# One rms per group applied to the branch product's sums instead of to the SSD rows

## The chip, the cores and the metric

The kernel runs on one core of a Trainium2 chip. The metric is the device time of one execution in microseconds (us). A core has TensorE (PE, matrix products into PSUM), VectorE (DVE), ScalarE (ACT), GpSimd (POOL) and SyncE (SP), whose queue issues the large DMA transfers. All engines work through their own instruction queues, and meet through semaphores.

## The reference

One layer of an encoder block on 256 tokens of width 1024, in float32. The input projection feeds a sparse-attention branch and a Mamba-2 (SSD) branch; both are gated, merged and projected, and a mixture of experts follows.

```python
y_ssd = ssd_chunked(xh, dt, A, bs, cs) + d_skip[:, None] * xh
y_ssd = gated_group_rmsnorm(y_ssd, z, ssd_norm)
merged = sigmoid(gate_a) * (y_attn @ w_attn_branch) + sigmoid(gate_b) * (y_ssd @ w_ssd_branch)
x = x + merged @ w_out
x = x + hier_moe(rmsnorm(x, ffn_norm), ...)

def gated_group_rmsnorm(y, z, g):
    yf = y * silu(z)
    yg = yf.reshape(*yf.shape[:-1], 4, 512)                  # 4 groups of 512 channels
    yg = yg * rsqrt(mean(yg * yg, axis=-1, keepdims=True) + EPS)
    return yg.reshape(yf.shape) * g
```

What matters here is the last function: each token has one root mean square (rms) per group of 512 channels, and the normed rows are multiplied by `w_ssd_branch` (2048 x 1024). The factor 1 / rms belongs to a token and a group, so it is the same for all 512 channels that a group brings into the product.

## The kernel before, in words

**Products in split halves.** Nearly every product up to the router is made with each float32 operand split into two parts of a shorter type, a hi part (ACT, `split_hi`, L152) and a lo part, the operand less its hi (`split_lo`, L156). A k-tile of 128 rows then takes three matmuls, hi x hi, hi x lo and lo x hi:

```python
PASSES = ((0, 0), (0, 1), (1, 0))
KSP = (0, 1, 0, 1)      # lo parts: k-tiles 0, 2 on DVE and 1, 3 on POOL, and so on
```

**Weights in chunks.** The weights stream through chunks of 8 k-tiles of 128 x 512 (or 128 x 256). `next_w()` keeps one chunk ahead: it puts the raw chunk on SP's queue in pieces of 512 KB and asks for the splits. The hi and lo pairs live in a ring of six buffers, so that splits run at most six k-tiles ahead of PE. `wide_chunk` (L294) makes one product of a wide chunk for both halves t of the tokens into two PSUM tiles, half 1 three k-tiles behind half 0.

**The SSD groups.** The four groups g of 512 channels come in two halves q of 256. While PE goes through the input-projection chunks of group g + 1, and in the end through two chunks of the attention branch (`ps_A`), it also makes the SSD products of group g: `ssd_x` and `ssd_e` prepare, `ssd_y` makes `py` on PE (L749, L752), adds the skip on DVE (L755) and multiplies by the gate (L756) into `yg`, squares it on ACT (L758) and sums the squares on POOL into `ysum` (L760 to L763). `ssd_tail` sums `ysum` over the partitions with `ps_n` on PE (L769), takes the power -1/2 (DVE L771, POOL L100), broadcasts 1 / rms over the partitions with a second product `ps_r` (PE, L775), multiplies `yg` by the norm's gain and by `ps_r` (DVE, L781, 16 in all), and splits the result into `yT` (ACT L783, DVE L784, 8 each), which is PE's stationary operand in the merge.

**The merge.** Four chunks of `w_ssd_branch`, for i (which two groups, 8 k-tiles) and c (which 512 output columns). Each gives two sums `ps_S`, one for each t, over all 8 k-tiles. DVE multiplies a sum by the gate (L832; the gate tile `tab[t, c][:, 1]` holds a tanh, and 1 is added on the way). For i = 0 POOL adds it to `tab[t, c][:, 0]`, which holds the gated attention product (L834); for i = 1 DVE adds (L836), PE transposes (L839), and ACT and DVE split into `mT` (L844, L845) for the output projection `ps_o`. The weight chunks are w31 to w34 in the merge, and w35 to w37 in the output projection.

**After that** come the norm, the router and 96 weight tiles of 1 MB for the experts (`we`), which `prefetch` (L270) puts on SP's queue as buffers come free, the first of them during the groups and the merge.

**Order.** The program is written in loops, and a scheduler then puts the instructions of each engine into one fixed order, by priorities (`HP` gives SSD steps theirs) and by its own estimates. A change in one place can therefore move instructions elsewhere in an engine's queue.

Of the kernel before, what the change touches and what calls it, by code (L numbers as in the profile page):

```python
# [11 lines left out]
F32 = mybir.dt.float32  # L12
# [8 lines left out]
P = 128  # L21
# [27 lines left out]
def block_kernel(ctx, tc, xin, idn, ngain, catt, cprep, cssd, cmoe, cwr, wsm, wwide, win, wgu, wdn, out, dbg=None):  # L49
# [633 lines left out]
    snorm = C("snorm")  # L683
    yT = [bigt([P, 2, 4, T], F32R, f"yT{g}") for g in range(4)]
# [53 lines left out]
    def ssd_y(g, q):  # L738
# [3 lines left out]
        st_[g, q, "yg"] = yg  # L742
# [3 lines left out]
        for h2 in range(2):  # L746
            py = paux.tile([P, T], F32, tag="x", name="py")
            for hh in range(2):
                pe.matmul(py[64 * hh:64 * hh + 64], lhsT=xdt[:, 0, 2 * h2 + hh, :], rhs=e0[h2][:, hh, :],  # L749
                          start=True, stop=False)  # L750
            for hh in range(2):
                pe.matmul(py[64 * hh:64 * hh + 64, P:T], lhsT=xdt[:, 1, 2 * h2 + hh, :],  # L752
                          rhs=e1[h2][:, hh, :], start=False, stop=True)
            ct = 4 * g + 2 * q + h2
            dve.scalar_tensor_tensor(yg[:, h2, :], xs[:, h2, :], hsk[:, ct:ct + 1], py, op0=ALU.mult, op1=ALU.add)  # L755
            dve.tensor_tensor(yg[:, h2, :], yg[:, h2, :], zs[:, h2, :], op=ALU.mult)  # L756
        sq = zs_t[g, q]
# [7 lines left out]
    def ssd_tail(g):  # L765
# [4 lines left out]
        r = ssd.tile([P, 2], F32, tag="nv", name="nv")  # L770
        dve.tensor_scalar(r, ps_n, 1.0 / 512, 4 * EPS, op0=ALU.mult, op1=ALU.add)  # L771
        power(r, r, None)
        ps_r = paux.tile([P, T], F32, tag="n", bufs=1, name="ps_r")
        for t in range(2):
            pe.matmul(ps_r[:, t * P:(t + 1) * P], lhsT=r[:, t:t + 1].to_broadcast([P, P]), rhs=ident,  # L775
                      start=True, stop=True)
        for q in range(2):
            yg = st_[g, q, "yg"]
            for b in range(2):
                ct = 4 * g + 2 * q + b  # L780
                dve.scalar_tensor_tensor(yg[:, b, :], yg[:, b, :], snorm[:, ct:ct + 1], ps_r, op0=ALU.mult, op1=ALU.mult)  # L781
            hl = yT[g][:, :, 2 * q:2 * q + 2]
            act.copy(hl[:, 0], yg)  # L783
            dve.tensor_sub(hl[:, 1], yg, hl[:, 0].bitcast(F32))  # L784
# [40 lines left out]

    for i in range(2):
        for c in range(2):
            ps = wide_chunk("S", yT[2 * i:2 * i + 2], LAG)
            for t in range(2):
                ta, tb = tab[t, c][:, 0], tab[t, c][:, 1]  # L830
                m = mo2.tile([P, 512], F32, tag="y", name="mg")
                dve.scalar_tensor_tensor(m, tb, 1.0, ps[t], op0=ALU.add, op1=ALU.mult)  # L832
                if i == 0:
# [477 lines left out]
```

## Time and profile before

| | |
|---|---|
| time, median of 3 runs | 583.62 us (583.45 to 583.9) |
| the profiled execution's own time | 585.1 us |
| its span in the profile | 583.3 us |
| PE busy | 552.6 us (95%), 3605 instructions |
| DVE busy | 330.9 us (57%), 689 |
| ACT busy | 271.8 us (47%), 633 |
| POOL busy | 239.5 us (41%), 254 |
| read from HBM | 157.54 MB, 272 GB/s over the span |

The shares are averages over stages that differ: the input projection and the attention up to about 185 us, the SSD groups up to 307.6, the merge up to 353, the output projection and router up to about 388, and then the experts. Matmuls are pipelined, so a busy PE is not PE at its peak; what its work costs is better read from one start to the next. Idle time of an engine that nobody waits for costs nothing.

### The profile page before, as it was taken

The page shows a single profiled execution, that of the slowest core. Times are in us where ns is not written, and L with a number is a line of the kernel's source. Part 1 is how long each engine was busy: PE and PEld are TensorE (multiplying, and loading weights), DVE is VectorE, ACT ScalarE, POOL GpSimd, SP SyncE. Part 2 cuts the span into 40 slices and gives each one's busy share as a digit, 9 for nine tenths or more (in the row PEclk, how much of TensorE's full clock was granted, in tenths as well). Part 3 has the DMA queues.
Part 4 walks back from the last instruction along what each step waited for, and adds up shares of the span by engine and source line. Part 5 has one row for each costly group of instructions (what it writes and reads, how often), then busy time and mean ns, then how long its engine had stood idle before and what let it go on. Part 6 is the DMA issues. An engine that isn't in the chain of part 4 may idle for free.

```text
span 583.3 us, 9898 instructions
## 1 busy us (share of the span) xinstructions
PE 552.6 (95%) x3605; PEld 400.6 (69%) x3605; DVE 330.9 (57%) x689; ACT 271.8 (47%) x633; POOL 239.5 (41%) x254
## 2 busy tenths in 40 slices
PE   8999989999999999999999999999998898988976
PEld 5878768798898999898878888964453452433512
DVE  3659975999996778989695657451111121111101
ACT  7567557757987877878764436410000000000001
POOL 4687584775844456656567745210000000000000
PEclk9999999999999999999999999999989997999989
DMA  7755244453435488645568589989999999999993
GB/s 272 250 162 169 103 147 146 144 174 124 128 122 186 149 323 334 217 149 185 208 194 300 177 307 389 405 344 417 419 417 408 420 417 421 409 415 421 420 407 123
DMA packets 35123, 159.27 MB, mean 273 GB/s; under 512 B 4096, under 2 KB 5760, under 8 KB 25856
## 3 DMA queue, kind: packets, MB, share of 16 engines
q1 hardware_dynamic: 33776, 157.30, 71.8%
q10 hardware_dynamic: 1296, 1.30, 0.7%
q8 instruction: 30, 0.49, 0.3%
q14 instruction: 21, 0.17, 0.1%
HBM read 157.54 MB, written 1.05 MB: 272 GB/s over the span
## 4 chain that ended last, share of the span: by engine, by line
PE 69%; DMA 12%; DVE 9%; issue 4%; POOL 3%; ACT 3%; SPq 0%; ACTq 0%; POOLq 0%; DVEq 0%
PE ps_S L294 8%; PE pgu L1037 6%; PE ps_xs L241 6%; PE ps_g L294 6%; DMA we<-wdn 5%; DMA we<-wgu 5%; PE ps_z L241 5%; PE py L1097 4%; PE ps_A L294 4%; PE acc L1112 4%; PE ps_g L1030 4%; PE ps_q L294 3%; PE ps_o L241 2%; PE ps_o L294 2%; PE ps_iq L294 2%
## 5 line engine op out<-in xcount | busy, mean ns | idle before, releaser
L156 POOL TENSOR_TENSOR w_hl<-w_raw,w_hl 128x512 fp32r<-128x512 f32 (+1 forms) x101 | 141.6, 1406 | 81.8 <-ACT w_hl L152 66.5
L152 ACT CAST w_hl<-w_raw 128x512 fp32r<-128x512 f32 (+1 forms) x212 | 125.7, 620 | 46.4 <-PE ps_S L294 18.5
L156 DVE TENSOR_TENSOR w_hl<-w_raw,w_hl 128x512 fp32r<-128x512 f32 (+1 forms) x111 | 100.4, 911 | 38.7 <-ACT w_hl L152 38.1
L1055 POOL TENSOR_TENSOR dc<-Dm,cmr 128x128 f32<-128x128 f32 x16 | 6.1, 401 | 143.5 <-DVE Dm L960 137.4
L1037 PE MATMUL pgu<-we,xg 128*32 128x512 f32 x512 | 60.2, 603 | 3.9 <-DMA we<-wgu 3.9
L241 PE MATMUL ps_z<-hT,w_hl 128*128 128x256 f32 x384 | 51.7, 286 | 0.0
L241 PE MATMUL ps_xs<-hT,w_hl 128*128 128x256 f32 x384 | 50.7, 285 | 0.0
L241 PEld LDWEIGHTS ps_z<-hT,w_hl 128*128 128x128 f32 x384 | 47.8, 190 | 2.0 <-issue 2.0
L241 PEld LDWEIGHTS ps_xs<-hT,w_hl 128*128 128x128 f32 x384 | 47.6, 191 | 2.1 <-issue 2.1
L294 PE MATMUL ps_g<-w_hl,gT 128*128 128x512 f32 x192 | 48.1, 399 | 0.0
L294 PE MATMUL ps_S<-w_hl,yT 128*128 128x512 f32 x192 | 44.6, 391 | 0.0
L1033 DVE TENSOR_TENSOR xg<-ps_g,cmoe 128x512 f32<-128x512 f32 (+2 forms) x18 | 11.3, 631 | 57.4 <-PE ps_g L1030 57.4
L1030 PEld LDWEIGHTS ps_g<-Dm,x_sb 128*128 128x128 f32 x256 | 31.0, 191 | 14.9 <-issue 9.7
L294 PEld LDWEIGHTS ps_g<-w_hl,gT 128*128 128x128 f32 x192 | 34.9, 188 | 9.3 <-DVE w_hl L156 1.0
L294 PEld LDWEIGHTS ps_S<-w_hl,yT 128*128 128x128 f32 x192 | 35.8, 188 | 7.4
L1037 PEld LDWEIGHTS pgu<-we,xg 128*32 128x32 f32 x512 | 15.1, 110 | 37.1 <-issue 26.1
L1097 PE MATMUL py<-we,aTt 128*32 128x512 f32 (+1 forms) x272 | 35.8, 616 | 3.8 <-DVE aTt L1083 2.1
L1108 ACT COPY y<-py 128x512 f32<-128x512 f32 (+1 forms) x9 | 4.8, 539 | 66.9 <-PE py L1097 66.9
L1075 DVE SCALAR_TENSOR_TENSOR ac<-th,pgu 128x256 f32<-128x256 f32 x8 | 3.4, 421 | 57.5 <-ACT th L1073 57.5
L1112 PE MATMUL acc<-y,dcT 128*128 128x512 f32 (+1 forms) x68 | 32.6, 606 | 0.9 <-DVE y L1110 0.8
L1030 PE MATMUL ps_g<-Dm,x_sb 128*128 128x128 f32 x256 | 33.4, 280 | 0.0
L1073 ACT ACTIVATE th<-pgu,rs 128x256 f32<-128x256 f32 x8 | 3.8, 474 | 55.1 <-PE pgu L1037 55.1
(296 smaller groups left out, 968.9 us busy)
## 6 DMA issues: line engine op xcount, KB each, us to landing
we<-wgu SPq DMA_DIRECT2D x55, 1024.0 KB, 13.8
w_raw<-wwide SPq DMA_DIRECT2D x60, 512.0 KB, 3.9
w_raw<-win SPq DMA_DIRECT2D x44, 512.0 KB, 3.9
we<-wdn SPq DMA_DIRECT2D x17, 1024.0 KB, 17.4
we<-wdn SPq DMA_DIRECT2D x28, 512.0 KB, 12.0
we<-wgu SPq DMA_DIRECT2D x18, 512.0 KB, 10.2
x_sb<-xin SPq DMA_DIRECT2D x2, 512.0 KB, 4.4
we<-wdn SPq DMA_DIRECT2D x4, 256.0 KB, 11.5
```

Of the source, the lines that this page charges most:

```text
L152: return act.copy(self.hl[i][:, 0], self.raw[i])
L156: return eng.tensor_sub(hl[:, 1], self.raw[i], hl[:, 0].bitcast(F32))
L241: pe.matmul(ps, lhsT=lhs[k][:, a], rhs=rhs[k][:, b], start=j == 0 and k == 0 and i == 0, stop=j == len(regions) - 1 and k == KD - 1 and i ...
L294: pe.matmul(ps[t], lhsT=lhs[t][k][:, a], rhs=w[k][:, b], start=k == 0 and i == 0, stop=k == KD - 1 and i == 2)
L1030: pe.matmul(ps[:, kk, :], lhsT=x1[:, t, (k + kk) * P:(k + kk + 1) * P], rhs=Dm[:, t].rearrange("p e j -> p (e j)"), start=t == 0, stop=t == 1)
L1033: dve.tensor_tensor(xg[:, ks, :], ps, fgain[:, ks].unsqueeze(2).to_broadcast([P, n, P]), op=ALU.mult)
L1037: i = pe.matmul(pgu[32 * e:32 * e + 32, :], lhsT=xg[:, k, 32 * e:32 * e + 32], rhs=wg[k][e], start=k == 0, stop=k == KD - 1, tile_position ...
L1055: pool.tensor_tensor(dc[:, t], Dm[:, t], cmr[:, t, 4 * q:4 * q + 4].unsqueeze(2).to_broadcast([P, 4, NSLOT]), op=ALU.mult)
L1073: act.activation(th, pgu[:, 0:256], AF.Tanh, scale=rs)
L1097: i_py = pe.matmul(py[32 * e:32 * e + 32, :], lhsT=aTt[:, f, 32 * e:32 * e + 32], rhs=wd[2 * n + f][e][:, c], start=f == 0, stop=f == 1, t ...
L1108: act.copy(y, py)
L1112: pe.matmul(acc[t][n][:, c], lhsT=dcT[:, t * P:(t + 1) * P], rhs=y, start=False, stop=q == 7 and c.stop == 512)
```

## The change

The rows of SSD enter the branch product without their 1 / rms. `ssd_y` makes the hi and lo parts straight from `yg` and the norm's gain, per 128 channels. `ssd_tail` keeps 1 / rms as `rg[:, g, t]`, one number for each token on its partition, and makes no broadcast. In the merge, each chunk's product is kept apart by group: two sums of 4 k-tiles in place of one of 8, the second in PSUM banks of the accumulators. DVE multiplies each by its `rg` and by the gate in one instruction, and POOL or DVE adds: 12 additions on POOL (4 before) and 4 on DVE (as before). So that one instruction can do it, the gate tiles get their 1 beforehand, by four instructions on POOL.

```diff
@@ -681,6 +681,7 @@
         dve.tensor_scalar(hsk, C("dskip"), 0.5, None, op0=ALU.mult)
 
     snorm = C("snorm")
+    rg = cst.tile([P, 4, 2], F32, name="rg")
     yT = [bigt([P, 2, 4, T], F32R, f"yT{g}") for g in range(4)]
 
 
@@ -739,7 +740,6 @@
         xs, zs, xdt = xs_t[g, q], zs_t[g, q], st_[g, q]
         e0, e1 = st_[g, q, "e"]
         yg = ssd.tile([P, 2, T], F32, tag="yg", name=f"yg{g}{q}", bufs=YB)
-        st_[g, q, "yg"] = yg
         if q == 0:
             st_[g, "ysum"] = ssd.tile([P, T], F32, tag="ysum", name="ysum", bufs=1)
         ysum = st_[g, "ysum"]
@@ -754,6 +754,13 @@
             ct = 4 * g + 2 * q + h2
             dve.scalar_tensor_tensor(yg[:, h2, :], xs[:, h2, :], hsk[:, ct:ct + 1], py, op0=ALU.mult, op1=ALU.add)
             dve.tensor_tensor(yg[:, h2, :], yg[:, h2, :], zs[:, h2, :], op=ALU.mult)
+
+        hl = yT[g][:, :, 2 * q:2 * q + 2]
+        for b in range(2):
+            ct = 4 * g + 2 * q + b
+            act.activation(hl[:, 0, b], yg[:, b], AF.Copy, scale=snorm[:, ct:ct + 1])
+            dve.scalar_tensor_tensor(hl[:, 1, b], yg[:, b], snorm[:, ct:ct + 1], hl[:, 0, b].bitcast(F32),
+                                     op0=ALU.mult, op1=ALU.subtract)
         sq = zs_t[g, q]
         act.activation(sq, yg, AF.Square)
         if q:
@@ -767,21 +774,9 @@
         ps_n = paux.tile([P, 2], F32, tag="n", bufs=1, name="ps_n")
         for t in range(2):
             pe.matmul(ps_n[:, t:t + 1], lhsT=ysum[:, t * P:(t + 1) * P], rhs=ones, start=t == 0, stop=t == 1)
-        r = ssd.tile([P, 2], F32, tag="nv", name="nv")
+        r = rg[:, g]
         dve.tensor_scalar(r, ps_n, 1.0 / 512, 4 * EPS, op0=ALU.mult, op1=ALU.add)
         power(r, r, None)
-        ps_r = paux.tile([P, T], F32, tag="n", bufs=1, name="ps_r")
-        for t in range(2):
-            pe.matmul(ps_r[:, t * P:(t + 1) * P], lhsT=r[:, t:t + 1].to_broadcast([P, P]), rhs=ident,
-                      start=True, stop=True)
-        for q in range(2):
-            yg = st_[g, q, "yg"]
-            for b in range(2):
-                ct = 4 * g + 2 * q + b
-                dve.scalar_tensor_tensor(yg[:, b, :], yg[:, b, :], snorm[:, ct:ct + 1], ps_r, op0=ALU.mult, op1=ALU.mult)
-            hl = yT[g][:, :, 2 * q:2 * q + 2]
-            act.copy(hl[:, 0], yg)
-            dve.tensor_sub(hl[:, 1], yg, hl[:, 0].bitcast(F32))
 
     def steps(g, names):
 
@@ -823,14 +818,32 @@
     xp = ctx.enter_context(tc.tile_pool(name="xp", bufs=NX, reuse_waits="tile"))
     pacc = ctx.enter_context(tc.tile_pool(name="pacc", bufs=1, space=PSUM, reuse_waits="tile"))
 
+    for t in range(2):
+        for c in range(2):
+            pool.tensor_scalar(tab[t, c][:, 1], tab[t, c][:, 1], 1.0, None, op0=ALU.add)
     for i in range(2):
         for c in range(2):
-            ps = wide_chunk("S", yT[2 * i:2 * i + 2], LAG)
-            for t in range(2):
+
+            w = pairs(next_w(), slice(0, 512))
+            src = pairs(yT[2 * i:2 * i + 2], slice(0, T))
+            pss = {}
+            for k in range(KD + LAG):
+                for t in range(2):
+                    kk = k - LAG * t
+                    if not 0 <= kk < KD:
+                        continue
+                    g = kk // 4
+                    if kk % 4 == 0:
+                        pss[t, g] = (pacc.tile([P, 512], F32, tag=f"acc{t}1", name="ps_S") if g
+                                     else pmm.tile([P, 512], F32, tag="mm", name="ps_S"))
+                    for a, b in PASSES:
+                        pe.matmul(pss[t, g], lhsT=src[kk][:, a, t * P:(t + 1) * P], rhs=w[kk][:, b],
+                                  start=kk % 4 == 0 and (a, b) == PASSES[0], stop=kk % 4 == 3 and (a, b) == PASSES[2])
+            for g, t in ((0, 0), (0, 1), (1, 0), (1, 1)):
                 ta, tb = tab[t, c][:, 0], tab[t, c][:, 1]
                 m = mo2.tile([P, 512], F32, tag="y", name="mg")
-                dve.scalar_tensor_tensor(m, tb, 1.0, ps[t], op0=ALU.add, op1=ALU.mult)
-                if i == 0:
+                dve.scalar_tensor_tensor(m, pss[t, g], rg[:, 2 * i + g, t:t + 1], tb, op0=ALU.mult, op1=ALU.mult)
+                if i == 0 or g == 0:
                     pool.tensor_add(ta, m, ta)
                     continue
                 dve.tensor_add(m, m, ta)
```

The scheduler then orders the engines anew. Three places of the new order follow.

PE around the last `ps_n`, in the merge. `yT_2054` and `yT_2055` are the first two groups before, `yT_2055` and `yT_2056` in the change. Before (28 merge matmuls stand ahead of the first row):

```order
L294 MATMUL ps_S<-w_hl,yT_2055 128x512 x8
L769 MATMUL ps_n<-ones,ysum 128x1 x2
L294 MATMUL ps_S<-w_hl,yT_2055 128x512 x12
L294 MATMUL ps_S<-w_hl,yT_2054 128x512 x12
L775 MATMUL ps_r<-ident,nv 128x128 x2
L294 MATMUL ps_S<-w_hl,yT_2055 128x512
L294 MATMUL ps_S<-w_hl,yT_2054 128x512 x6
```

and in the change (the first row is the first merge matmul):

```order
L840 MATMUL ps_S<-w_hl,yT_2055 128x512
L749 MATMUL py<-e_3810,xdt_3775 64x256 x2
L840 MATMUL ps_S<-w_hl,yT_2055 128x512 x3
L752 MATMUL py<-e_3810,xdt_3775 64x128 x2
L840 MATMUL ps_S<-w_hl,yT_2055 128x512 x20
L776 MATMUL ps_n<-ones,ysum 128x1 x2
L840 MATMUL ps_S<-w_hl,yT_2055 128x512 x4
L840 MATMUL ps_S<-w_hl,yT_2056 128x512 x24
L840 MATMUL ps_S<-w_hl,yT_2055 128x512 x16
```

The last `ps_n` follows 36 merge matmuls before and 24 in the change, and no `ps_r` comes after it.

POOL from the last power on. `w32` and `w33` are the second and third merge chunk; the number behind `hl` tells the k-tile buffers apart, and `tab_692`, `tab_694`, `tab_1004`, `tab_1006` are the merge's four tiles. Before:

```order
L100 TENSOR_TENSOR nv_3947<-nv_3947,mhalf_80 128x2
L834 TENSOR_TENSOR tab_692<-mg_4059,tab_692 128x512
L156 TENSOR_TENSOR w32_hl_3990<-w32_raw_3981,w32_hl_3990 128x512
L834 TENSOR_TENSOR tab_694<-mg_4062,tab_694 128x512
L156 TENSOR_TENSOR w32_hl_3992<-w32_raw_3983,w32_hl_3992 128x512
L156 TENSOR_TENSOR w33_hl_4074<-w33_raw_4065,w33_hl_4074 128x512
L156 TENSOR_TENSOR w33_hl_4076<-w33_raw_4067,w33_hl_4076 128x512
L834 TENSOR_TENSOR tab_1004<-mg_4147,tab_1004 128x512
L156 TENSOR_TENSOR w33_hl_4078<-w33_raw_4069,w33_hl_4078 128x512
L834 TENSOR_TENSOR tab_1006<-mg_4150,tab_1006 128x512
```

and in the change:

```order
L100 TENSOR_TENSOR rg_2054<-rg_2054,mhalf_80 128x2
L847 TENSOR_TENSOR tab_692<-mg_4050,tab_692 128x512
L847 TENSOR_TENSOR tab_694<-mg_4053,tab_694 128x512
L847 TENSOR_TENSOR tab_692<-mg_4056,tab_692 128x512
L156 TENSOR_TENSOR w32_hl_3977<-w32_raw_3968,w32_hl_3977 128x512
L156 TENSOR_TENSOR w32_hl_3979<-w32_raw_3970,w32_hl_3979 128x512
L847 TENSOR_TENSOR tab_694<-mg_4059,tab_694 128x512
L156 TENSOR_TENSOR w32_hl_3981<-w32_raw_3972,w32_hl_3981 128x512
L156 TENSOR_TENSOR w33_hl_4071<-w33_raw_4062,w33_hl_4071 128x512
L847 TENSOR_TENSOR tab_1004<-mg_4146,tab_1004 128x512
L847 TENSOR_TENSOR tab_1006<-mg_4149,tab_1006 128x512
L156 TENSOR_TENSOR w33_hl_4073<-w33_raw_4064,w33_hl_4073 128x512
```

The first three additions stand together ahead of two splits, and 6 of the 11 rows behind the power are additions, where 4 of 9 were.

POOL's next rows, up to the output projection's first splits (`w35`). Before:

```order
L156 TENSOR_TENSOR w33_hl_4080<-w33_raw_4071,w33_hl_4080 128x512
L156 TENSOR_TENSOR w34_hl_4162<-w34_raw_4153,w34_hl_4162 128x512
L156 TENSOR_TENSOR w34_hl_4164<-w34_raw_4155,w34_hl_4164 128x512
L156 TENSOR_TENSOR w34_hl_4166<-w34_raw_4157,w34_hl_4166 128x512
L156 TENSOR_TENSOR w34_hl_4168<-w34_raw_4159,w34_hl_4168 128x512
L156 TENSOR_TENSOR w35_hl_4274<-w35_raw_4265,w35_hl_4274 128x512
L156 TENSOR_TENSOR w35_hl_4276<-w35_raw_4267,w35_hl_4276 128x512
L156 TENSOR_TENSOR w35_hl_4278<-w35_raw_4269,w35_hl_4278 128x512
```

and in the change:

```order
L847 TENSOR_TENSOR tab_1004<-mg_4152,tab_1004 128x512
L156 TENSOR_TENSOR w33_hl_4075<-w33_raw_4066,w33_hl_4075 128x512
L847 TENSOR_TENSOR tab_1006<-mg_4155,tab_1006 128x512
L156 TENSOR_TENSOR w33_hl_4077<-w33_raw_4068,w33_hl_4077 128x512
L847 TENSOR_TENSOR tab_692<-mg_4242,tab_692 128x512
L156 TENSOR_TENSOR w34_hl_4167<-w34_raw_4158,w34_hl_4167 128x512
L847 TENSOR_TENSOR tab_694<-mg_4245,tab_694 128x512
L156 TENSOR_TENSOR w34_hl_4169<-w34_raw_4160,w34_hl_4169 128x512
L156 TENSOR_TENSOR w34_hl_4171<-w34_raw_4162,w34_hl_4171 128x512
L156 TENSOR_TENSOR w34_hl_4173<-w34_raw_4164,w34_hl_4173 128x512
L156 TENSOR_TENSOR w35_hl_4287<-w35_raw_4278,w35_hl_4287 128x512
L847 TENSOR_TENSOR tab_1004<-mg_4362,tab_1004 128x512
```

Six more additions stand between the splits of `w33`, `w34` and `w35`. The second split of the fourth chunk (`w34_hl_4167` is its k-tile 1) is the 17th row from the first addition on.

The four instructions that add 1 to the gates (L823) stand in POOL's queue in the attention stage, between splits of `w8` to `w10`. No row of SP's queue moves by more than a few places, and the order of the experts' transfers is the same.

## Rows read from the trace of the kernel before

**Rows 1.** Busy time of each engine by stage: us, busy (instructions), PEclk, DMA share, GB/s

```profile
150.00:307.60 157.60, 157.44 (x1192) 140.28 (x1191) 136.11 (x270) 123.23 (x294) 94.52 (x83) 1.00 0.58 203
307.60:342.00 34.40, 34.40 (x157) 28.51 (x156) 21.23 (x31) 16.64 (x28) 24.26 (x20) 1.00 0.71 234
...
353.00:388.00 35.00, 34.74 (x237) 29.86 (x236) 21.33 (x68) 15.62 (x43) 11.42 (x11) 1.00 1.01 407
388.00:392.00 4.00, 4.00 (x32) 2.08 (x32) 0.75 (x3) 0.00 (x0) 0.76 (x2) 1.00 0.55 168
```

**Rows 2.** Chain of waits, in order of time, its last row: start, us, what

```profile
541.82 19.88 DMA we<-wgu
```

**Rows 3.** TensorE's timeline: start, us, engine, line, operation, tile, count

```profile
236.28 0.71 PE L775 MATMUL ps_r<-ident,nv 128*128 128x128 f32 x4
236.92 0.43 PE L749 MATMUL py<-e,xdt 128*64 128x256 f32 x1
...
315.83 0.50 PE L769 MATMUL ps_n<-ones,ysum 128*128 128x1 f32 x4
...
321.78 0.61 PE L775 MATMUL ps_r<-ident,nv 128*128 128x128 f32 x4
322.14 25.90 PE L294 MATMUL ps_S<-w_hl,yT 128*128 128x512 f32 x113
...
353.07 5.83 PE L294 MATMUL ps_o<-w_hl,mT 128*128 128x512 f32 x24
```

**Rows 4.** Groups of instructions, 185 to 353 us: busy us, mean ns, idle before

```profile
L756 DVE TENSOR_TENSOR yg<-yg,zs 128x256 f32<-128x256 f32 x16 | 10.1, 632 | 0.2
...
L784 DVE TENSOR_TENSOR yT<-yg,yT 128x512 fp32r<-128x512 f32 x8 | 7.8, 974 | 0.3 <-ACT yT L783 0.3
...
L781 DVE SCALAR_TENSOR_TENSOR yg<-yg,cssd,ps_r 128x256 f32<-128x256 f32 x16 | 6.6, 473 | 0.1
...
L834 POOL TENSOR_TENSOR tab<-mg,tab 128x512 f32<-128x512 f32 x4 | 5.6, 1400 | 1.8 <-DVE mg L832 1.8
...
L783 ACT CAST yT<-yg 128x512 fp32r<-128x512 f32 x8 | 5.1, 637 | 0.9 <-DVE yg L781 0.9
...
L832 DVE SCALAR_TENSOR_TENSOR mg<-tab,ps_S 128x512 f32<-128x512 f32 x6 | 3.9, 679 | 1.7 <-PE ps_S L294 1.7
```

**Rows 5.** GpSimd's timeline, 305 to 356 us: start, us, idle before and its releaser

```profile
311.95 0.73 POOL L761 TENSOR_TENSOR ysum<-ysum,zs 128x256 f32<-128x256 f32 x1
...
318.04 0.71 POOL L100 TENSOR_TENSOR nv<-nv,mhalf 128x2 f32<-128x2 f32 x1
...
331.68 1.29 POOL L834 TENSOR_TENSOR tab<-mg,tab 128x512 f32<-128x512 f32 x1 [1.23 <-DVE mg L832]
332.92 1.29 POOL L156 TENSOR_TENSOR w_hl<-w_raw,w_hl 128x512 fp32r<-128x512 f32 x1
...
336.13 1.30 POOL L156 TENSOR_TENSOR w_hl<-w_raw,w_hl 128x512 fp32r<-128x512 f32 x1 [0.67 <-ACT w_hl L152]
...
351.59 1.30 POOL L156 TENSOR_TENSOR w_hl<-w_raw,w_hl 128x512 fp32r<-128x512 f32 x1 [3.08 <-DMA w_raw<-wwide]
```

**Rows 6.** VectorE's timeline, 305 to 342 us

```profile
319.18 0.68 DVE L156 TENSOR_TENSOR w_hl<-w_raw,w_hl 128x512 fp32r<-128x512 f32 x1
319.78 0.68 DVE L832 SCALAR_TENSOR_TENSOR mg<-tab,ps_S 128x512 f32<-128x512 f32 x1
...
336.94 1.04 DVE L156 TENSOR_TENSOR w_hl<-w_raw,w_hl 128x512 fp32r<-128x512 f32 x1 [0.89 <-ACT w_hl L152]
```

**Rows 7.** Groups of instructions in the merge, 307.6 to 353 us, GpSimd and VectorE

```profile
L156 POOL TENSOR_TENSOR w_hl<-w_raw,w_hl 128x512 fp32r<-128x512 f32 x15 | 20.4, 1361 | 14.4 <-ACT w_hl L152 11.3 <-DMA w_raw<-wwide 3.1
...
L156 DVE TENSOR_TENSOR w_hl<-w_raw,w_hl 128x512 fp32r<-128x512 f32 x15 | 13.4, 899 | 15.5 <-ACT w_hl L152 15.5
```

**Rows 8.** GpSimd's timeline in the attention stage

```profile
109.59 1.30 POOL L484 TENSOR_TENSOR h<-gT 128x512 f32<-128x512 f32 x1 [0.36 <-DVE sc L451]
```

**Rows 9.** TensorE's timeline in the attention stage

```profile
146.17 0.66 PE L519 MATMUL ps_s<-kT,qT 128*128 128x128 f32 x4 [0.85 <-DVE mx L523]
```

## The prediction

> **What bounds the kernel now.** I read the busy times by stage first [rows 1]. From 150 to 342 us TensorE (PE) works 157.44 of 157.60 us and 34.40 of 34.40, while VectorE (DVE) works 136.11 and 21.23, ScalarE (ACT) 123.23 and 16.64, GpSimd (POOL) 94.52 and 24.26, and the DMA share is 0.58 and 0.71. In the SSD groups and the merge, then, PE alone sets the pace. From 353 on the DMA share is 1.01, except in 388 to 392 us, where it falls to 0.55 at 168 GB/s: the ring of weight buffers is full, and transfers go on only as PE's first expert products free them. The chain of waits [rows 2] ends in the transfer of expert weights. So the end is the moment at which PE reaches the experts, plus a stream. Anything that shifts PE before 353 us shifts that moment one to one, and so the end; a gain is cut off once the dip at 388 is closed, a delay is not. The dip lacks 0.45 of 4 us, that is 1.8 us, so about that much can be gained on the far side and a little beyond it by the stream's earlier start.
>
> The sum is made against the profiled execution's own 585.1 us, which is 1.5 above the median of 583.62; the result is carried over by that difference. A change of 0.2%, about 1.2 us, is what a measurement of this kernel can tell from none.
>
> **What PE loses.** The four broadcasts of 1 / rms (ps_r, two matmul instructions and four records each) vanish. From the start of one to the start of what follows, PE spent 236.92 - 236.28 = 0.64 us on the first and 322.14 - 321.78 = 0.36 on the last [rows 3]; the four come to 2.09. The term is **-2.1**, at least -1.4 (four of the shortest).
>
> **Work that moves in the groups.** DVE loses 16 products with ps_r (6.6 us) and 8 subtractions of 128x512 (7.8), and gains 16 fused products of 128x256 with two SBUF operands; the nearest row, L756, has 632 ns, so 10.1 us [rows 4]. DVE gains 4.3 us. ACT loses 8 casts of 637 ns and gains 16 of half the width: between 0 and 5.1 us more. Both lie beside a PE that had no gap [rows 1], so I cost them at nothing. If that cover were gone, DVE's 4.3 would come back as a gain.
>
> **The last ps_n.** The order puts 24 merge matmuls ahead of it instead of 36, 12 x 0.228 = 2.7 us less (25.90 us for 113 of them [rows 3], whose last runs out beside the next: 0.228 each). Before, ysum was complete at 311.95 + 0.73 = 312.68 [rows 5], 3.15 ahead of ps_n at 315.83 [rows 3]. ACT now makes a hi part between the last product and its square, at most 0.64 more. The slack is about zero, and a wait at PE is possible: **+0.2**, from 0 to one POOL add of 0.73.
>
> **The merge.** Eight more products out of PSUM on DVE (0.679 each, 5.4 us) and eight more additions on POOL (1.40 each by their mean, 1.25 back to back as 331.68 to 332.92 shows; 10 to 11.2 us) [rows 4, 5]. PE itself does the same 192 matmuls. The question is whether the splits of the weights still arrive in time, since POOL makes half of them and its additions stand among them in its queue.
>
> POOL and DVE do not run freely beside each other here. A DVE split of 128x512 takes 0.69 when POOL is idle (319.18, and its successor starts 0.60 later), but the one at 336.94 takes 1.04 and ends at 337.98, which is 0.55 after POOL's split of 336.13 ended at 337.43: it did its work once POOL was through [rows 5, 6]. The group means of 899 ns on DVE and 1361 on POOL [rows 7] say that this is common. DVE's product with PSUM and one SBUF operand keeps its 0.68 throughout (L832).
>
> So I lay out one queue of POOL work and DVE splits from the last ps_n on. The square root needs, as before, until 318.04 + 0.71 = 318.75, 2.9 after ps_n [rows 5]; one product adds 0.7: POOL's first addition starts at 3.6. Up to the split of the fourth chunk's second k-tile the new order has nine additions and eight splits on POOL, 17 x 1.25 = 21.25, and DVE has ten splits of 0.6 and a small operation of 0.3, 6.3 in all. That ends at 31.2. PE needs the tile 128 matmuls after ps_n: 0.36 + 128 x 0.228 = 29.5. PE is late by 1.6. The bounds: if DVE's splits fit between POOL's work without holding it, 3.6 + 21.25 = 24.9, wait 0; if all of POOL's operations take the mean of 1.40, 3.6 + 23.8 + 6.3 = 33.7, wait 4.2. I take the middle, **+1.6**, because the overrun at 336.94 is nearest to the serial reading, while the back-to-back row excludes that every operation takes the mean.
>
> The Trainium skill, page "SBUF — State Buffer", section "Who interferes with whom", gives the serial reading as a rule: a VectorE instruction with two SBUF inputs takes the port that GpSimd reads through, and the one that comes later waits out the whole of the other. It speaks against this change, which replaces products out of PSUM by ones with two SBUF inputs and adds GpSimd reads. By it the sum is the one above; the trace's 0.55 us after POOL's end agrees. A sharing of the port with both merely slower would give the mean of 1.40, the upper end.
>
> **Between merge and output projection.** Before, PE went from its last merge matmul to 24 of the output projection at 353.07 [rows 3] and only then to the second set of transposes. The new order takes 20, and needs a sum on DVE that follows POOL additions 11 and 12; those stand behind the split of the output weights that at 351.59 had waited 3.08 us for its transfer [rows 5]. I take **+0.3**, from 0 to 1.0 (four matmuls of 0.228 earlier).
>
> **Adding 1 to the gates.** Four one-operand POOL instructions of 128x512, once per gate tile, go into the attention stage. No row shows one; the bounds are 0 and a two-operand operation's 1.30 [rows 8]. POOL has idle time there, but the top-k and softmax steps on DVE end three waits of PE, the longest 0.85 before 146.17 [rows 9], and one such instruction can hold a DVE step in that chain. **+0.3**, from 0 to 1.3.
>
> **Sum:** -2.1 + 0.2 + 1.6 + 0.3 + 0.3 = +0.3, 585.4 in the profiled execution; carried to the median, **583.9 us**. This case alone, with a wait of 0.7 to 2.5 in the merge, reaches from 583.0 to 584.8.
>
> **The rivals.**
>
> **A, faster:** POOL is ahead all the way, its queue ends at 24.9 against PE's 29.5. For it: POOL had 10 us to spare in 34.4 [rows 1], and PE waited for no split before. Against it: the long DVE splits. The merge's 1.6 goes: -1.3, or 582.3; with every wait at zero -2.1, 581.5.
>
> **B, slower:** POOL paces the merge. It decides as soon as the queue runs over 2.5 us behind PE's schedule: that, with the 0.8 of the three other waits, is the broadcasts' 2.1 and 1.2 more. Then PE waits 4.2 at the fourth chunk: -2.1 + 4.2 + 0.8 = +2.9, 586.5. For it: the means in [rows 7]. Against: additions that stand back to back, 1.25.
>
> **C, slower by the gates:** one of the four instructions holds up the attention chain by its whole 1.3 in place of 0.3: +1.3, 584.9. POOL's idle time there speaks against it.
>
> **D, the change does more than it says:** PE's pace in the groups is really that of DVE, whose busy time there is 86% [rows 1], through deadlines that the trace gives to nobody. The 4.3 us of DVE come on top: -4.0, 579.6. PE's missing gaps speak against it. That the change removes no PE work is excluded by the order, which has no ps_r left.
>
> **How the numbers follow.** Forecast 0.44, A 0.30, B 0.17, C 0.05, D 0.04. The forecast's own case is within 0.2% in 0.38 of its 0.44 and slower in 0.06. A is faster in 0.26 and within 0.2% in 0.04; B and C are slower; D is faster. That makes faster 0.30, same 0.42, slower 0.28. The range goes from 581.6, which takes in nearly all of A, to 586.4, which takes in most of B and leaves its tail and D outside: under 2 in 10.
>
> **What the changed profile would show.** Right: no ps_r on PE, and merge matmuls starting some 1.5 us earlier; then one wait of PE for a weight split that POOL made, 1 to 2 us, in the last merge chunk, and POOL busy near 38 of the merge's 45 us, where it had 20.4 of splits, 5.6 of additions and some 2 of small operations, and gets 10 more. DVE's fused products of 128x256 near 630 ns. A right: the merge without any PE wait, and experts reached 1 to 2 us earlier. B right: several PE waits for POOL's splits from the third chunk on. C right: new PE waits in the softmax between 105 and 150 us. The prediction would be wrong if PE's waits in the groups were unequal to those before, or if the end did not follow PE's arrival at the experts.

## The result, and the profile after

The changed kernel takes 589.6 us (median of 6 runs, 587.36 to 591.03); the kernel before took 583.99 beside it (6 runs). The medians lie 5.6 us apart; the ratio over all executions is 1.0086, 95% interval 1.0063 to 1.0109, about 5.0 us slower, where 583.9 us and no change were forecast, and outside the range of 581.6 to 586.4.

The profiled execution took 590.08 us, 588.3 of it span. The first fence is from the page: the span and each engine's busy time. The second is the busy time by stage, with the columns of [rows 1].

```profile
span 588.3 us, 9903 instructions
...
PE 553.8 (94%) x3589; PEld 400.1 (68%) x3589; DVE 344.9 (59%) x689; ACT 271.7 (46%) x641; POOL 263.5 (45%) x266
```

```profile
150.00:305.74 155.74, 154.51 (x1160) 137.09 (x1158) 138.44 (x266) 123.09 (x297) 92.50 (x80) 1.00 0.58 203
305.74:342.00 36.26, 35.38 (x160) 28.16 (x159) 28.52 (x33) 16.17 (x28) 33.70 (x26) 1.00 0.66 221
342.00:353.00 11.00, 11.00 (x54) 8.79 (x52) 6.42 (x7) 2.89 (x6) 7.08 (x6) 1.00 1.00 394
353.45:362.93 9.48, 7.05 (x33) 4.89 (x32) 9.34 (x14) 5.08 (x11) 8.40 (x6) 1.00 0.96 356
362.93:386.88 23.95, 23.14 (x171) 21.56 (x170) 9.60 (x22) 10.35 (x31) 7.34 (x8) 0.99 0.96 378
386.88:396.00 9.12, 9.12 (x55) 5.25 (x56) 5.84 (x41) 0.48 (x3) 0.76 (x2) 0.85 0.65 248
```

Most of the loss is waiting, and 1.2 us more is a stretch at a lower clock, told below. The worst stretch is the hand-over from the merge to the output projection: in 9.48 us PE works 7.05 while DVE works 9.34. Before, DVE worked 5.64 in this stretch and PE 6.71 of its 6.73 us:

```profile
353.07:359.80 6.73, 6.71 (x33) 5.17 (x31) 5.64 (x10) 3.55 (x8) 4.47 (x3) 1.00 0.99 401
```

PE's timeline of the changed kernel shows where (start, us, ..., idle before and its releaser):

```profile
184.06 1.94 PE L544 MATMUL po<-PT,v_sb 128*64 128x512 f32 x8
...
224.41 2.77 PE L241 MATMUL ps_xs<-hT,w_hl 128*128 128x256 f32 x21 [0.56 <-DVE zs L703]
...
305.74 0.40 PE L840 MATMUL ps_S<-w_hl,yT 128*128 128x512 f32 x1
306.06 0.65 PE L749 MATMUL py<-e,xdt 128*64 128x256 f32 x4
...
313.63 0.61 PE L776 MATMUL ps_n<-ones,ysum 128*128 128x1 f32 x4 [0.88 <-POOL ysum L768]
...
353.45 3.46 PE L294 MATMUL ps_o<-w_hl,mT 128*128 128x512 f32 x14
357.40 1.65 PE L294 MATMUL ps_o<-w_hl,mT 128*128 128x512 f32 x6 [0.49 <-DVE w_hl L156]
...
362.55 0.63 PE L852 MATMUL ps_mT<-ident,mg 128*128 128x128 f32 x4 [1.80 <-DVE mg L849]
362.93 1.66 PE L294 MATMUL ps_o<-w_hl,mT 128*128 128x512 f32 x6
...
383.74 1.15 PE L924 MATMUL ps_lg<-cwr,xT 128*128 128x36 f32 x8 [0.35 <-ACT xT L920]
...
385.60 1.48 PE L924 MATMUL ps_lg<-cwr,xT 128*128 128x36 f32 x8 [0.46 <-ACT xT L920]
386.88 3.88 PE L880 MATMUL ps_w<-on 128*128 128x512 bf16 x11
...
393.85 1.07 PE L1050 MATMUL pgu<-we,xg 128*32 128x512 f32 x8
```

Before, the same places of PE's timeline read as follows, from the end of the attention to the first expert product:

```profile
184.72 1.94 PE L544 MATMUL po<-PT,v_sb 128*64 128x512 f32 x8
...
358.75 1.03 PE L839 MATMUL ps_mT<-ident,mg 128*128 128x128 f32 x8
359.80 1.42 PE L294 MATMUL ps_o<-w_hl,mT 128*128 128x512 f32 x5
...
382.51 2.54 PE L867 MATMUL ps_w<-on 128*128 128x512 bf16 x11
...
388.26 1.07 PE L1037 MATMUL pgu<-we,xg 128*32 128x512 f32 x8
```

Executions start this part up to 3 us apart (183.18 to 186.09), so I measure from the last attention product (`po`). Steps are differences of starts; "rows alone" and "two repairs" are experiments told below.

| PE's way, us | before | after | after less before | rows alone, less before | two repairs, less before |
|---|---|---|---|---|---|
| last `po` to first `ps_S` (SSD groups) | 122.91 | 121.68 | -1.23 | -1.09 | -1.25 |
| to first `ps_o` (merge) | 45.44 | 47.71 | +2.27 | +0.89 | +2.31 |
| to `ps_o` behind the last transposes (hand-over) | 6.73 | 9.48 | +2.75 | -0.22 | +1.14 |
| to `ps_w` (rest of the projection, router) | 22.71 | 23.95 | +1.24 | +0.03 | -0.23 |
| to first `ps_rk` (11 `ps_w`) | 2.50 | 3.72 | +1.22 | 0.00 | +0.01 |
| to first `pgu` (experts) | 3.25 | 3.25 | 0.00 | 0.00 | -0.01 |
| sum | 203.54 | 209.79 | **+6.25** | **-0.39** | **+1.97** |

In the first two lines some 0.96 us have only changed sides: the last `py` products now stand behind the first merge matmul (306.06). Of the merge's +2.27, 0.88 is the wait at `ps_n`. From `pgu` to the end of the span it is 195.04 before and 194.45 after; with the 0.66 by which this execution left the attention earlier, 6.25 - 0.66 - 0.59 = 5.0, the difference of the spans.

**The merge** had no wait of PE for a weight split. The queue that the forecast laid out is here in three rows of POOL's timeline, the first addition, the 17th operation and what follows:

```profile
317.31 4.25 POOL L847 TENSOR_TENSOR tab<-mg,tab 128x512 f32<-128x512 f32 x3
...
341.43 1.74 POOL L156 TENSOR_TENSOR w_hl<-w_raw,w_hl 128x512 fp32r<-128x512 f32 x1
343.13 1.28 POOL L847 TENSOR_TENSOR tab<-mg,tab 128x512 f32<-128x512 f32 x1
```

It began 3.68 after `ps_n`, as laid out (3.6). Its 17 operations took until 343.17, 1.52 us each, 29.5 us after `ps_n` (forecast 31.2). PE came for the tile 128 matmuls after 314.09: in the trace's records the 129th starts at 343.22. The tile was in time by 0.05 us, so this queue had no slack either.

**The hand-over** on DVE, after; `mg<-ps_S` at 353.02 and 354.02 takes up the last chunk's first two sums, which PE had finished by about 347:

```profile
347.83 1.77 DVE L156 TENSOR_TENSOR w_hl<-w_raw,w_hl 128x512 fp32r<-128x512 f32 x1
352.41 0.70 DVE L156 TENSOR_TENSOR w_hl<-w_raw,w_hl 128x512 fp32r<-128x512 f32 x1 [2.81 <-ACT w_hl L152]
353.02 0.74 DVE L845 SCALAR_TENSOR_TENSOR mg<-ps_S,rg,tab 128x512 f32<-128x512 f32 x1
...
354.02 0.74 DVE L845 SCALAR_TENSOR_TENSOR mg<-ps_S,rg,tab 128x512 f32<-128x512 f32 x1
...
357.27 1.78 DVE L849 TENSOR_TENSOR mg<-mg,tab 128x512 f32<-128x512 f32 x1
358.97 0.74 DVE L845 SCALAR_TENSOR_TENSOR mg<-ps_S,rg,tab 128x512 f32<-128x512 f32 x1
359.63 1.10 DVE L156 TENSOR_TENSOR w_hl<-w_raw,w_hl 128x512 fp32r<-128x512 f32 x1
360.65 1.75 DVE L849 TENSOR_TENSOR mg<-mg,tab 128x512 f32<-128x512 f32 x1
```

and on POOL and ACT, where the first split of w35 waits for its transfer:

```profile
352.98 1.30 POOL L156 TENSOR_TENSOR w_hl<-w_raw,w_hl 128x512 fp32r<-128x512 f32 x1 [3.92 <-ACT w_hl L152]
354.23 2.57 POOL L847 TENSOR_TENSOR tab<-mg,tab 128x512 f32<-128x512 f32 x2
356.76 5.09 POOL L156 TENSOR_TENSOR w_hl<-w_raw,w_hl 128x512 fp32r<-128x512 f32 x3
```

```profile
351.76 1.14 ACT L152 CAST w_hl<-w_raw 128x512 fp32r<-128x512 f32 x2 [5.14 <-DMA w_raw<-wwide]
```

The two sums lay ready for some 6 us, and DVE stood idle for 2.81 of them, because a split that waited for a transfer stood ahead in its queue. Then everything came at once: sums, splits and final additions beside POOL's splits, and the final additions took 1.78 and 1.75 us each; before, two of them took 1.78 together, and ended at 358.19. Before, DVE was also full there, 4.00 of 4.00 us from 354 to 358, and the transposes at 358.75 came only 0.56 us behind its last addition. The first row is from DVE's timeline before, the others are busy times as above:

```profile
356.41 1.78 DVE L836 TENSOR_TENSOR mg<-mg,tab 128x512 f32<-128x512 f32 x2
...
354.00:358.00 4.00, 4.00 (x18) 3.08 (x17) 4.00 (x6) 2.01 (x4) 2.99 (x2) 1.00 1.00 418
358.00:362.00 4.00, 3.98 (x22) 3.10 (x22) 2.36 (x6) 2.46 (x7) 1.86 (x2) 1.00 1.04 418
```

So the hand-over hung on DVE without a gap in PE to tell it.

**The clock.** From 386.88 the 11 `ps_w` took 3.72 instead of 2.50. The windows of the changed kernel show the granted clock (third column from the end):

```profile
384.00:386.00 2.00, 1.54 (x14) 1.30 (x13) 0.62 (x3) 0.63 (x2) 0.00 (x0) 1.00 1.03 420
386.00:388.00 2.00, 2.00 (x10) 1.32 (x10) 1.25 (x9) 0.00 (x0) 0.00 (x0) 0.55 1.02 414
388.00:390.00 2.00, 2.00 (x7) 0.75 (x6) 1.65 (x15) 0.00 (x0) 0.00 (x0) 0.60 1.06 418
```

The waits of 0.35 and 0.46 at 383.74 and 385.60 stand ahead of it. Near 0.5 means that most of these 4 us ran at 1.2 GHz. The Trainium skill, page "TensorE: Matmul & The Clock Gate", section "What's actually happening", says that the clock follows how busy TensorE has been lately; the order of these rows agrees.

### The profile page after: what moved, and what is told of

Same layout as the page of the kernel before. It is cut to its first block, busy times and chain, and to the rows that moved or that the text cites. A ratio compares the mean times of both kernels' runs of the same rounds, so it can differ in the third digit from the quotient of the medians.

```text
span 588.3 us, 9903 instructions
## 1 busy us (share of the span) xinstructions
PE 553.8 (94%) x3589; PEld 400.1 (68%) x3589; DVE 344.9 (59%) x689; ACT 271.7 (46%) x641; POOL 263.5 (45%) x266
## 3 DMA queue, kind: packets, MB, share of 16 engines
HBM read 157.54 MB, written 1.05 MB: 270 GB/s over the span
## 4 chain that ended last, share of the span: by engine, by line
PE 52%; DVE 18%; DMA 14%; issue 5%; ACT 5%; POOL 4%; ACTq 0%; POOLq 0%; DVEq 0%; SPq 0%
DMA we<-wgu 9%; PE ps_S L840 7%; DMA we<-wdn 5%; PE pgu L1050 5%; DVE w_hl L156 4%; PE py L1110 3%; PE ps_z L241 3%; PE ps_g L1043 3%; PE ps_xs L241 3%; PE acc L1125 3%; PE ps_q L294 2%; PE ps_g L294 2%; DVE acc L603 2%; PE ps_o L241 2%; PE ps_iq L294 2%
## 5 line engine op out<-in xcount | busy, mean ns | idle before, releaser
L156 POOL TENSOR_TENSOR w_hl<-w_raw,w_hl 128x512 fp32r<-128x512 f32 (+1 forms) x101 | 145.7, 1449 | 65.5 <-ACT w_hl L152 53.2
L152 ACT CAST w_hl<-w_raw 128x512 fp32r<-128x512 f32 (+1 forms) x212 | 124.1, 620 | 49.6 <-DMA w_raw<-wwide 19.5
L156 DVE TENSOR_TENSOR w_hl<-w_raw,w_hl 128x512 fp32r<-128x512 f32 (+1 forms) x111 | 105.3, 959 | 24.7 <-ACT w_hl L152 24.2
L1125 PE MATMUL acc<-y,dcT 128*128 128x512 f32 (+1 forms) x68 | 30.7, 577 | 0.1
```

The lines of the kernel that those rows point to most:

```text
L152: return act.copy(self.hl[i][:, 0], self.raw[i])
L156: return eng.tensor_sub(hl[:, 1], self.raw[i], hl[:, 0].bitcast(F32))
L1125: pe.matmul(acc[t][n][:, c], lhsT=dcT[:, t * P:(t + 1) * P], rhs=y, start=False, stop=q == 7 and c.stop == 512)
```

## The experiments

Four theories. **Q**: POOL's longer queue paces PE. **V**: the longer chain of steps per sum costs that much in any order. **O**: the new order of the groups and of the router's end, with the clock, makes the loss. **H**, the hand-over, was named after the first four runs: the loss comes from the order of the queues around 347 to 386 us, where ready work stands behind splits that wait, DVE has no room, and the router's last products come late. "PE's way" below is the sum of the table above, less that of before (203.54).

| kernel | ratio to before | 95% interval | PE's way |
|---|---|---|---|
| the change | 1.0086 | 1.0063 to 1.0109 | +6.25 |
| second half's additions on DVE | 1.0136 | 1.0076 to 1.0195 | +7.40 |
| sum before gate | 1.0071 | 1.0047 to 1.0095 | +4.56 |
| rows part alone, twice | 1.0006; 0.9982 | 0.9993 to 1.0019; 0.9967 to 0.9997 | -0.39; -0.39 |
| merge part alone | 1.0098 | 1.0072 to 1.0124 | +5.76 |
| splits behind sums | 1.0066 | 1.0042 to 1.0091 | +2.70 |
| and transposes pinned | 1.0085 | 1.0050 to 1.0120 | +5.08 |
| three repairs | 1.0052 | 1.0034 to 1.0071 | +4.38 |
| router end alone | 1.0074 | 1.0051 to 1.0097 | +3.29 |
| four repairs | 1.0032 | 1.0018 to 1.0046 | +1.92 |
| two repairs | 1.0028 | 1.0011 to 1.0046 | +1.97 |

The way is that of one profiled execution; the ratio is over all executions of both kernels and need not be that of the medians (1% is 5.8 us). So a shorter way does not always show in the ratio.

### Second half's additions on DVE

```diff
-                    pool.tensor_add(ta, m, ta)
+                    (dve if i else pool).tensor_add(ta, m, ta)
```

> The change, with the four additions of the first group of the last two merge chunks (i = 1, g = 0) on VectorE in place of GpSimd. Theory Q (GpSimd's longer queue delays the last weight splits and the sums that the output projection needs): the queue before the output projection is four additions (about 5 us) shorter, the waits of TensorE there (0.49 + 1.80 us in the changed kernel) shrink under 1 us, time 585.5 to 587.5. Rival V (the longer chain of steps per sum on VectorE is what is late, whoever adds): the waits stay at 2 us or grow, 589 to 591.

Slower still: the median is 591.53, above both ranges. PE's waits: 1.18 for a split of DVE at 358.31, 0.93 for `mg` at 361.80, 1.44 for a split of DVE at 364.58, and a clock of 0.57 from 364 to 368. Relieving POOL at the expense of DVE makes it worse: Q falls, DVE is short at the hand-over.

### Sum before gate

```diff
+                rgt = rg[:, 2 * i + g, t:t + 1]
+                if g == 0:
+                    ms[t] = mo2.tile([P, 512], F32, tag="y", name="mg")
+                    act.activation(ms[t], pss[t, g], AF.Copy, scale=rgt)
+                    continue
+                m = ms[t]
+                dve.scalar_tensor_tensor(m, pss[t, g], rgt, m, op0=ALU.mult, op1=ALU.add)
+                dve.scalar_tensor_tensor(m, tb, 1.0, m, op0=ALU.add, op1=ALU.mult)
```

> Unscaled rows as in the change, but the two sums of a chunk are joined first (ScalarE scales the first out of PSUM, VectorE adds the second with its scale) and then gated once, so that GpSimd has four additions as before the change, and no additions of 1 to the gates. Theory Q: no waits of TensorE at the start of the output projection, and the gain at the merge's start of 1.9 us is kept: 581.5 to 583.5. Rival V (one VectorE step more after the last sum than before the change): a wait of 1 to 2 us before the last transposes stays, 584 to 586.

POOL has as few additions as before, and the kernel is still slower than before: Q falls again. PE waits 0.75 and 1.18 for `mg` (DVE) at 359.95 and 361.76, 1.9 us as V had it; but the median of 588.17 is above V's range too. Behind these waits the clock falls (PE's timeline, and a window of its 2 us):

```profile
362.22 4.51 PE L294 MATMUL ps_o<-w_hl,mT 128*128 128x512 f32 x12
```

```profile
362.00:364.00 2.00, 2.00 (x8) 1.55 (x7) 0.90 (x2) 1.40 (x4) 0.00 (x0) 0.52 0.97 410
```

Fourteen such matmuls took 3.46 us at 353.45 in the change, 0.25 each; these twelve would be 3.0 us and took 4.5.

### Rows part alone, and merge part alone

The first takes only the new `ssd_y` and `ssd_tail` and leaves the merge as it was; it leaves out 1 / rms. The second scales the rows as before, fills `rg` with ones and takes the merge of the change. This is its edit to the kernel before, up to the merge:

```diff
+    rg = cst.tile([P, 4, 2], F32, name="rg")
+    pool.memset(rg, 1.0)
...
```

> The row part alone: rows unscaled, no broadcast of 1 / rms, the merge as before the change; the factor 1 / rms is left out of the result. Theory Q: the loss is all in the merge part, so this is before less the broadcasts, 581.0 to 582.5. Rival O (the new order of the groups and of the router's end, and the clock, make the loss): 584 or more.

> The merge part alone: rows scaled and split as before the change, with the broadcasts; the merge in two sums a chunk with a factor of 1 from a tile of ones. Theory Q: the loss without the gain, 588.5 to 592. Rival O: under 587.

Nearly all of the loss is in the merge part, +5.76 (median 589.94, in Q's range), with waits in the same two places as in the change: 0.34 and 1.05 for `mg`, 0.35 and 0.46 in the router, `ps_w` to `ps_rk` 4.04; 0.83 for a split in the merge stands in place of the change's 0.49 for one in the hand-over. The rows part is worth -0.39 on PE's way; its ratio is 1.0006, and its median of 584.50 lies in O's range, not in Q's. O falls by the merge part alone, though the router's end and the clock, which it names, are in that loss. The two parts' ways add up to 5.37; the change's wait of 0.88 at `ps_n` is in neither. A second measurement asked whether the gain is real:

> The row part alone again (the factor 1 / rms is left out of the result), for a second profile: in the first one TensorE reached the experts 1.1 us earlier than before and the last weights landed 1.1 us earlier, but the stretch behind them was 1.4 us longer at the low clock. If that stretch differs from execution to execution, the new profile has another clock there and a time that goes with it, and the median is 0.5 to 1.0 us below before. If the gain is always eaten there, the median is within 0.3 us of before.

0.9982 (median 583.75, 1.04 below that of before), and PE's way again -0.39, although this execution left the attention 2 us later (186.09 against 184.00). From `pgu` to the end it took 195.56, in the first one 195.95, before 195.04: more than the gain is lost there in both. The row part is a gain of some tenths of a microsecond on PE's way; between 1.0006 and 0.9982 the runs don't say how much of it reaches the end.

### Splits behind sums

The splits of w35 are asked for behind the sums, additions and transposes that are ready earlier (`issue_after` puts what follows behind the instruction named):

```diff
+            late = (i, c) == (1, 1)
+            w = pairs(next_w(late), slice(0, 512))
...
+                    if late and t:
+                        with tc.issue_after(i_m.ins), tc.issue_after(i_a.ins), tc.issue_after(i_h.ins), tc.issue_after(i_l.ins):
+                            wready[-1].split(KSP)
```

> The change, with the splits of the output projection's first weight chunk (w35) queued behind the first sums and the transposes' results of the merge on VectorE, ScalarE and GpSimd. In the changed kernel those sums were complete on TensorE at about 347 us and were taken up at 353.0 and 354.0, behind a split that waited for its transfer until 352.4. Theory H (the hand-over: work that is ready stands in the queues behind splits that wait for a transfer, and VectorE then has more than the 24 matmuls of cover can hide): the first sums of the last chunk are taken up by 349 us, TensorE waits under 0.8 us in 353 to 364 us (2.3 in the changed kernel), 584.5 to 587. Rival V (the longer chain of steps per sum is late in any order): 1.5 us or more of waits there, 588 to 590.

On DVE's timeline and PE's: DVE now takes up the two sums 4.3 us earlier, 0.9 of it an earlier start of the execution, and PE waits 0.35 for `mg` where it waited 1.80:

```profile
348.72 0.74 DVE L847 SCALAR_TENSOR_TENSOR mg<-ps_S,rg,tab 128x512 f32<-128x512 f32 x1
...
349.72 0.73 DVE L847 SCALAR_TENSOR_TENSOR mg<-ps_S,rg,tab 128x512 f32<-128x512 f32 x1
```

```profile
359.65 0.63 PE L857 MATMUL ps_mT<-ident,mg 128*128 128x128 f32 x4 [0.35 <-DVE mg L854]
360.50 1.88 PE L295 MATMUL ps_o<-w_hl,mT 128*128 128x512 f32 x7 [0.22 <-DVE mT L863]
```

The hand-over falls from 9.48 to 7.85 us (before 6.73), with the same arithmetic: this share of the loss is H's. The router's waits stay. The median of 587.95 misses H's range, and V's by 0.05: it gains less than this execution does, which is the fastest of ten (585.77 to 591.37), and by the ratio this repair alone is not clear of the change.

### And transposes pinned

```diff
+                        i_o = o_half(0)
...
+                    if late:
+                        st.enter_context(tc.issue_after(i_o.ins))
```

> As the run before this one, and TensorE's transposes of the last chunk are queued behind the 24 matmuls of the output projection that do not need them, as in the kernel before. Theory H: no wait of TensorE over 0.3 us in 353 to 364 us, no fall of the clock there, 583.0 to 585.5, about the kernel before (its row part alone gave no gain either). Rival V: waits of 1 us or more before the transposes, 587 to 589.

A miss, with a median of 589.69 above both ranges: with 24 output matmuls ahead of the transposes by order, the scheduler pulled narrow `ps_o` products forward, ahead of their own splits, and PE waited 1.44 for DVE's split at 361.91. One pin moved the wait to another place.

### Router end alone

```diff
+                    with tc.issue_after(hf_at[1].ins):
+                        mm3(regions[1:2], range(0, 6))
+                    with tc.issue_after(hf_at[2].ins):
+                        mm3(regions[1:2], range(6, KD))
```

> The change with only the router's end put back as in the kernel before. Theory H: the waits at the start of the output projection stay (2 us or more in 353 to 364 us), those of 0.35 and 0.46 us at the router's end go; 1 to 2.4 us less than the changed kernel, 587 to 588.5. If the waits at the start of the output projection were all the loss, 589 to 590.

In the change, the last narrow products stood ahead of the router's; this puts them between its steps, as before. The wait of 1.80 stays, at 362.03. Only 0.24 is left of the router's waits, as before, and `ps_w` runs at full clock: 385.32 to 387.82, 2.50. The way is 2.96 shorter than the change's (0.70 of it in the hand-over, where the wait of 0.49 is gone), but the time is not: the median of 589.64 misses H's range and lies in the one for the case that the waits at the start of the output projection were all the loss. In the profiled execution the stretch from `pgu` to the end took 197.3 us, 2.9 more than in the change, at a mean clock of 0.95 against 0.97. That the router's end costs PE its share is shown; that it costs time is not shown by this run.

### Three, four and two repairs

The three repairs are the two above and the squares ahead of the hi and lo parts, for `ps_n`'s wait of 0.88.

> The run with the splits of w35 behind the sums, and two repairs more: the squares are made before the hi and lo parts (the last ps_n had waited 0.88 us for them), and at the router's end the transposes of x stand among the last matmuls of the output projection as they do in the kernel before. Theory H (the loss is three places where the new order puts ready work too late or too early, and what the clock does after each wait): no wait of TensorE over 0.4 us between 300 us and the experts, from the first merge matmul to the first expert matmul at most 81.5 us (88.1 in the changed kernel, 80.6 before, where 1.3 us of py lie ahead of it), 582.5 to 585. Rival V (the summation by group costs on its own): 586 or more.

H's range is missed, and V's 586 or more holds (median 588.04). `ps_o` to `ps_w` is nearly as short as before (29.97 against 29.44; 33.43 in the change). But DVE's splits came later: PE waited 0.71 for `ysum` and 1.29 for a split at 314.05, and ran at the lower clock from 314 to 320, here by the window:

```profile
314.00:316.00 2.00, 1.95 (x5) 1.56 (x6) 1.38 (x3) 0.00 (x0) 2.00 (x3) 0.50 0.98 315
```

The four leave the squares as in the change and put the last `ps_n` behind 36 merge matmuls in place of 24; the two leave `ps_n` alone:

> All repairs of the order, none of the arithmetic: the splits of w35 behind the sums, the router's end as in the kernel before, and the last ps_n behind 36 merge matmuls in place of 24 (the squares stand where the change has them; putting them first had brought a wait of 1.29 us for a split and the low clock). Theory H: no wait of TensorE over 0.4 us from the first merge matmul to the experts, that stretch 81.5 us or less after taking off 1.3 us of py (80.6 before), 583 to 585. Rival V (the summation by group costs on its own): 586.5 or more.

> As the run before this one, with the last ps_n where the change has it, behind 24 merge matmuls: theory H expects the wait of 0.88 us for the sum of squares there, and 0.9 to 1.4 us more than the run with all repairs, 584.5 to 586; rival V sees no difference between the two.

Both end at +0.3%, with medians of 586.80 (in V's range, not in H's) and 586.20 (just above H's). Moving `ps_n` took its wait away, and 0.33 for POOL's split came in its place (316.03): no difference, as V had it. The two repairs keep 0.90 at `ps_n` and 0.33 at the hand-over; their router is as fast as before (PE's timeline of the two repairs):

```profile
313.33 0.61 PE L777 MATMUL ps_n<-ones,ysum 128*128 128x1 f32 x4 [0.90 <-POOL ysum L769]
...
360.19 0.63 PE L857 MATMUL ps_mT<-ident,mg 128*128 128x128 f32 x4 [0.33 <-DVE mg L854]
...
383.52 2.54 PE L885 MATMUL ps_w<-on 128*128 128x512 bf16 x11
```

**What follows.** The order of the queues accounts for about two thirds of the loss: with the same arithmetic the ratio goes from 1.0086 to 1.0028, with intervals that do not meet, and PE's way from +6.25 to +1.97. By the intervals the share lies between a third and all of it. H's times were missed in all six runs that had one, and what it said of the waits held in part; so the share rests on the comparison of these two kernels, not on H's forecasts. For the last third V is right so far: against the rows part alone, two repairs are 2.36 us longer, 1.42 of it in the merge (0.90 the wait at `ps_n`) and 1.36 in the hand-over on DVE, less 0.26 in the router and 0.16 in the groups. No order that I tried frees it, and whether one could stays open. No version that computes the whole function beat the kernel before.

## Why the prediction was wrong

- **What bounds the kernel: right.** PE came to the experts 5.59 later by the clock of the span, and the span is 5.0 longer.
- **PE loses ps_r, -2.1: right in itself, but given back.** From start to next start, the four broadcasts held 2.09 us of PE's time before. In the rows part alone, whose way is -0.39, PE's timeline between `po` and `pgu` gives back 0.42 in waits, 0.6 at the 32 `ps_b` and 0.6 at the `ps_x`, which stand in another order among the same other products; the 192 merge matmuls take 0.3 more from start to start, and 0.7 more in the change. Why these take longer there wasn't tried.
- **Work beside PE in the groups, 0: not quite.** "Beside a PE that had no gap" was the argument; the new order has one gap of 0.56 at 224.41, for DVE's `zs`. It is in all kernels with the rows part and in none without. An unequal wait in the groups was one of the prediction's own signs of being wrong. DVE's fused products, taken as 632 ns each, took 746.
- **The last ps_n, +0.2 with 0.73 at most: 0.88.** The slack was taken as zero; 0.33 of the wait is the last addition into `ysum`, which took 1.06 and not 0.73, and 0.55 was missing without it.
- **The merge, +1.6: 0.** The queue was laid out rightly but sized by a strictly serial reading; it ended 1.7 earlier, and PE came for the tile 0.05 later. Rival A's wait of zero came about, but not for A's reason: the queue ended at 29.5 and not at 24.9. A wait of zero by so little is partly luck. B's several waits did not come.
- **Between merge and output projection, +0.3 from 0 to 1.0: this is the step that failed.** It measured +2.75. Behind it came +1.24 in the router and +1.22 by the clock, for which the sum had no term. I counted the four matmuls less of cover, and saw that DVE and POOL had a split of w35 in their queues that waits for its transfer. What I did not count is that ready work, two sums finished at 347, would stand behind it, that DVE was full from 354 to 358 already, and that the transposes at 358.75 were just in time. A PE without waits looked like slack; there was at most 0.56 us of it. With the splits put behind the sums, the same arithmetic made this stretch 7.85 instead of 9.48.
- **The gates, +0.3: a little less than 0.** The additions cost 1.66 to 1.95 us each on POOL, more than the 1.30 that I took for the upper end, and were hidden: from PE's `ps_q` behind its wait for POOL, at 78.30 (78.39 after), to `po` it is 106.42 before and 105.67 after, and in the experiments 106.14 to 106.21 with them and 106.42 to 106.43 without. PE's three waits for `mx`, 1.7 us in all with that of [rows 9], are gone; two others of 0.6 and 0.5 stand in that stage.
- **POOL against DVE: the serial reading, in part.** In the merge a DVE split took 1288 ns in the mean (899 in [rows 7]) and POOL's 1568 (1361). `mg<-mg,tab`, with two SBUF operands, took 1.78 beside POOL's splits, while the product out of PSUM kept its 0.74. That agrees with the rule of the Trainium skill that the prediction named, page "SBUF — State Buffer", section "Who interferes with whom". The rule bore on the hand-over, where I did not apply it.

## What to carry to other kernels

Where the bounding engine has no wait, follow the engine that hands it its next operand through that stage, and ask how late each of its pieces is ready: 100% busy next to 100% busy is no slack. An instruction that waits for a transfer holds up ready work behind it in its queue; a change that puts more ready work there needs its order looked at first. Take a saving of PE's work as net only after the new order's starts are compared stage by stage.

## What the runs showed of the hardware

Short waits can be followed by a lower clock, and then cost more than their length. Behind waits of 0.35 and 0.46 (the change), 0.75 and 1.18 (sum before gate), 0.71 and 1.29 (three repairs), the granted clock fell to between 0.50 and 0.63 for some 4 to 6 us, at a price of 1.2 us in the first and 1.5 in the second; behind waits of 0.34 and 0.46 in the splits behind sums it did not (`ps_w` to `ps_rk` 2.51), nor behind the 1.80 of the change (1.00 from 362 to 368). What decides between them stays open. One kernel's executions differ as well: of the ten of that kernel, those with a mean clock of 0.987 or more took 585.77 to 587.48 us, those with 0.985 or less 588.42 to 591.37. In the 14 executions of the kernel before that stand beside the first experiments, clock and time do not go together: 0.985 took 584.25 us, and 0.993 took 584.22 and 584.53. The clock at the expert stage's end differs too, in kernels that differ little there: 0.86 from 556 to 568 before, and 0.57 from 560 to 572 with the router's end alone.
